# A decoder layer on one core: merge and output projection with tokens as rows and 512 weight columns as the moving side, attention values by tokens, and a ring of expert weights in three parts

## The chip, the core and the metric

The kernel runs on one core of a Trainium2 chip. The metric is the device time of one execution in microseconds. The engines are PE (TensorE, matrix products, with its weight loads shown apart as PEld), DVE (VectorE), ACT (ScalarE), POOL (GpSimd) and SP (SyncE, which here issues the DMA transfers). PSUM is the memory that products accumulate in.

## What is computed

One layer of a decoder with batch 1, 256 tokens and 1024 channels, in float32. Three token mixers run side by side, are merged by gates and projected; a mixture of 32 experts follows. Cut to what matters here:

```
cols = h @ w_in            # columns for the three mixers and three gates
y_a = rglru_branch(...)    # gated linear recurrence ("LRU")
y_b = stick_breaking_attention(q, k, v)      # 8 heads of 128
y_c = rwkv7_branch(...)    # delta-rule recurrence, 16 heads of 64
g_a, g_b, g_c = split(sigmoid(gate_logits))
merged = g_a * (y_a @ p_lru) + g_b * (y_b @ p_sb) + g_c * (y_c @ p_rwkv)
x = x + g_mix * (merged @ w_out)
h = modulate(rmsnorm(x), ...)
x = x + g_ffn * sum over the top 4 of 32 experts of
        weight * (clamped_swiglu(h @ w_gu[e]) @ w_down[e])
return rmsnorm(x)
```

The weights of the 32 experts are 384 MB (256 pieces of 1 MB for gate and up, 128 for down), those of everything ahead of them about 100 MB.

## The kernel before

All weights lie in DRAM in pieces that one DMA transfer brings in. `load` (L137) fetches one projection's weights of 1024 x 256 as two `raw` pieces of 512 KB each, into a pool of seven buffers (NRAW). A product with float32 accuracy is made of three: `split_w` (L146) splits a `raw` piece into a high part `whi` (a rounding copy on ACT, L149) and a low part `wlo` (a subtraction on DVE, L150), three buffers each (NSP); the activations come split as well (`hhi`/`hlo` for the normed input, `ybhi`/`yblo`, `yah`/`yal`, `ychi`/`yclo` for the three branches, `mh`/`ml` for the merged tile). high x high, high x low and low x high are then accumulated.

`proj` (L160) makes 256 output channels from 1024 input channels: the weights are the stationary operand (128 x 128), the 256 tokens move, 48 products (L168). The result has channels as partitions. Its accumulator is `mm`, one of three PSUM buffers of 512 columns (`pmm`, L157). `pch` (L175) gives one of three other buffers, `ch`; the rwkv recurrence and its output use these, and `tp` has two.

The program is written stage by stage: norm and adaLN, rwkv projections and the rwkv recurrence in two halves of 128 tokens, attention in four pairs of heads (`attention_pair`, L650), the LRU branch, the merge, output projection, router, experts. The written order is not the order in which an engine runs: a scheduler places each instruction ahead of time on its engine by data readiness, priorities and buffers that come free, with costs of its own; the engine then runs its list in that order and waits where an operand or a buffer isn't there. So the second half of the rwkv recurrence can stand, piece by piece, among the projections of other stages.

The second half's recurrence runs as follows, with the lines of its steps:
- 64-column triangular steps on DVE (L464, L465), a copy on ACT (L466), transposes on DVE (L469, L472);
- four groups of 32 x 32 products for the inverse blocks (L477, L483), copied by ACT and DVE (L479, L485);
- four steps over blocks of 32 tokens, each: `z` from the state and the block (L501, L504), its copy `rhs` on ACT (L507), `sps` on PE (L511), its copy `sav` on ACT (L512), `z` again and the state's update `nps` on PE (L515, L520), the copy `yt` on ACT (L529) and the new state `st` on DVE (L525 to L528);
- a group norm on DVE and ACT (L541 to L552), then for each of four column tiles two transposes (L557) and a product (L563) into `ch`, and three DVE operations that give `yc` (L559 to L564).

Attention (L611) turns the value tile of one head to tokens with two transposes and a DVE copy `vt`, as its values come out of `proj` with channels as partitions.

The merge (L860 to L891) runs over three branches (attention, LRU, rwkv) and four groups of 256 channels: gate projection from `hhi`/`hlo`, sigmoid on ACT into `gsig` (L878), projection of the branch, and a DVE product into `acc` (L881, or L883 and L884 for the later branches). In the third branch the sum is split into `mh`/`ml`. The output projection (L894 to L924) has four groups of 256 channels; there the merged tile is the stationary operand and the weights move, so that tokens are partitions; behind each group stand the gating and the residual add on DVE, the squares for the norm on ACT, and transposes and products for the router.

The experts' weights go through a ring of 19 buffers of 1 MB, opened in four parts of 7, 6, 3 and 3 (NR, L819; `ring_open`, L827) as the memory of earlier stages comes free. `ew_ahead` (L847) puts a few loads among those of the merge, in SP's queue. An expert makes `pg` and `pu` (L1043) on PE from gathered tokens `xe`, then the activation, then `pd` (L1070). At the end a count is read back (`values_load`, L1253), which decides whether a spare path must run.

Of the kernel before, what the change touches and what calls it, by code (L numbers as in the profile page):

```python
# [19 lines left out]
S = 256  # L20
# [60 lines left out]
def trace(tc, pools, I, out, dbg, stop):  # L81
# [63 lines left out]

    def split_w(src):  # L146

        hi, lo = (wsp.tile([128, 4, 256], F32R, name=n, tag=n, bufs=NSP) for n in ("whi", "wlo"))
# [501 lines left out]
    def attention_pair(pr):  # L650
        qkv = []
        for i, o in enumerate((OFF_Q, OFF_K, OFF_V)):
# [4 lines left out]
            ps = proj(raw, h2)  # L657
            A.activation(t, ps, AF.Copy, scale=128.0 ** -0.5 if i == 0 else 1.0)
            qkv.append(t)
        for cc in range(2):  # L660
            with sooner(HP_ATT):
                attention(pr * 2 + cc, *[t[:, cc] for t in qkv])
# [156 lines left out]
    NR = (7, 6, 3, 3)  # L819
    nload = [0]  # L820
# [18 lines left out]
    def ew(src):  # L839
        t = ew_tile()  # L840
        SY.dma_start(t.rearrange("p (k n) -> p k n", k=src.shape[1]), src)
# [15 lines left out]
    mhl, KS = None, 1  # L857
    EW = (0, 0, 1, 1, 1, 1, 1, 2)
    acc = [l4("acc") for _ in range(4)]
    for br, (yhl, pw) in enumerate(((ybhl, "p_sb"), (yahl, "p_lru"), (None, "p_rwkv"))):  # L860
        gcol = OFF_GATE + (1024, 0, 2048)[br]
# [5 lines left out]
        for pr in range(4):  # L867
            raw_g, raw_p = load(w_in, gcol + pr * 256), load(I[pw], pr * 256)
            if br:
                ew_ahead(EW[br * 4 + pr - 4])  # L870
            if br == 2 and pr == KS:
# [4 lines left out]
            c2 = slice(pr * 2, pr * 2 + 2)  # L876
# [3 lines left out]
            if br == 0:  # L880
                V.tensor_tensor(acc[pr], ps, sg, ALU.mult)  # L881
            else:
                V.tensor_tensor(sg, ps, sg, ALU.mult)  # L883
                V.tensor_tensor(acc[pr], acc[pr], sg, ALU.add)  # L884
            if br == 2:
                split_x(acc[pr], mhl[0][:, c2], mhl[1][:, c2])
                if pr == 3:
                    sqrt_ahead(sg)
# [4 lines left out]
    sqp = keep.tile([128, 2, 4], F32, name="sqp")  # L893
    lps = pch([128, 2, NE], "lps")  # L894
    for pr in range(4):
        raw = load(I["w_out"], pr * 256)
        ew_ahead(2 if pr < NR[1] - 4 else 1)
        ps = pmm().rearrange("p (t c) -> p t c", t=2)
        for q in range(2):
            hi, lo = split_w(raw[q])  # L900
            for t in range(2):
                for k in range(4):
                    for i, (w, x) in enumerate(((hi, 0), (hi, 1), (lo, 0))):
                        T.matmul(ps[:, t], mhl[x][:, q * 4 + k, t * 128:t * 128 + 128], w[:, k],
                                 start=(q + t + k + i == 0), stop=(q * 4 + k == 7 and i == 2), skip_group_check=True)
        if pr == 3:
# [3 lines left out]
        csl = slice(pr * 256, pr * 256 + 256)  # L910
        if pr == 2:
            gmix = mt("gmix", [128, 512])
            row_bcast(adag[:, 4:8], gmix)
        for t in range(2):
            V.tensor_tensor(ps[:, t], ps[:, t], gmix[:, pr % 2 * 256:pr % 2 * 256 + 256], ALU.mult)
# [412 lines left out]
```

## Time and profile before

| | us |
|---|---|
| Median of 3 runs | 1560.66 |
| Fastest and slowest run | 1560.38, 1562.57 |
| The profiled execution's own time | 1559.59 |
| Its span in the trace | 1557.8 |
| PE busy | 1455.1 (93%) |
| DVE busy | 643.3 (41%) |
| ACT busy | 413.3 (27%) |
| DMA moved | 498.87 MB, mean 320 GB/s |

The span is the time from the first to the last instruction of the profiled execution; some 2 us lie around it. The busy time of PE is a share of the whole; in the first 600 us and in the experts' part different things limit the kernel, so stretches are to be read one by one. A row of the timeline gives the start in us, the time it took, the engine, the line, the operation, output and inputs, and, in square brackets, for how long the engine had been idle and what released it.

### The profile page before, as it was taken

Reading aid. Unit: us, or ns where it says so; the run is one execution under the profiler, and the core shown is the slowest. Engines: PE = TensorE matmul, PEld = TensorE weight load, DVE = VectorE, ACT = ScalarE, POOL = GpSimd, SP = SyncE. Lnnn points to the kernel's source line nnn. Section 1 sums busy time; section 2 is a strip of 40 time slices with the busy share of each in tenths; the row PEclk is TensorE's granted clock in tenths of the full one; section 3 lists DMA queues with packets and bytes.
Section 4 is the critical chain, followed back from the end, with each engine's and each line's share of the span. In section 5 each row is a group of like instructions: output and inputs, shape, how many; then the busy total and the mean of one; then the engine's idle time right before and its main releaser. Section 6 shows DMA issues by size and latency. Waiting matters only on the chain. (4 is left out here: it accounts for less than half of the span.)

```text
span 1557.8 us, 21164 instructions
## 1 busy us (share of the span) xinstructions
PE 1455.1 (93%) x8608; PEld 830.7 (53%) x8608; DVE 643.3 (41%) x1330; ACT 413.3 (27%) x728; POOL 11.0 (1%) x59
## 2 busy tenths in 40 slices
PE   6998999899899998999999989999999989989896
PEld 4887989688899996334333324333323323323232
DVE  5678536589745764213232114213113113212313
ACT  4743335678534443001001001001001001001101
POOL 0000000000000000000000000000000000000000
PEclk8999799899899998999999999999999999999999
DMA  9554335246233777899999999999999999999994
GB/s 380 177 190 133 131 129 197 94 145 222 96 109 119 298 273 310 368 421 421 421 421 422 420 422 422 421 421 421 422 421 420 422 421 421 422 421 421 421 422 171
DMA packets 85558, 498.87 MB, mean 320 GB/s; under 512 B 12496, under 2 KB 12752, under 8 KB 36304
## 3 DMA queue, kind: packets, MB, share of 16 engines
q1 hardware_dynamic: 85456, 497.46, 80.0%
q8 instruction: 70, 1.15, 0.3%
q14 instruction: 32, 0.26, 0.0%
HBM read 496.37 MB, written 1.05 MB: 319 GB/s over the span
## 5 line engine op out<-in xcount | busy, mean ns | idle before, releaser
L1043 PE MATMUL pg<-ew,xe 128*64 128x512 f32 x1024 | 269.4, 603 | 25.2 <-DMA ew<-in_w_gu_dram 25.2
L1043 PE MATMUL pu<-ew,xe 128*64 128x512 f32 x1024 | 263.2, 595 | 0.0
L1070 PE MATMUL pd<-ew,act 128*64 128x512 f32 x992 | 231.6, 604 | 23.8 <-ACT act L1062 23.8
L168 PE MATMUL mm<-hhi,whi 128*128 128x256 f32 x720 | 212.6, 295 | 5.7 <-ACT gq L714 3.0
L168 PE MATMUL mm<-hhi,wlo 128*128 128x256 f32 x720 | 211.2, 293 | 1.1 <-DVE wlo L150 1.1
L168 PE MATMUL mm<-hlo,whi 128*128 128x256 f32 x720 | 211.7, 294 | 0.0
L150 DVE TENSOR_TENSOR wlo<-raw,whi 128x1024 fp32r<-128x1024 f32 x122 | 148.9, 1223 | 96.4 <-ACT whi L149 95.3
L149 ACT ACTIVATE whi<-raw 128x1024 fp32r<-128x1024 f32 x122 | 129.1, 1059 | 126.5 <-PE mm L168 94.4
L1043 PEld LDWEIGHTS pg<-ew,xe 128*64 128x64 f32 x1024 | 68.4, 137 | 174.1 <-issue 108.7
L1070 PEld LDWEIGHTS pd<-ew,act 128*64 128x64 f32 x992 | 69.7, 138 | 152.9 <-issue 116.0
L1043 PEld LDWEIGHTS pu<-ew,xe 128*64 128x64 f32 x1024 | 74.0, 137 | 143.3 <-issue 143.2
L168 PEld LDWEIGHTS mm<-hhi,whi 128*128 128x128 f32 x720 | 142.5, 198 | 12.8 <-issue 3.8
L168 PEld LDWEIGHTS mm<-hhi,wlo 128*128 128x128 f32 x720 | 142.2, 197 | 7.8 <-issue 5.2
L168 PEld LDWEIGHTS mm<-hlo,whi 128*128 128x128 f32 x720 | 142.3, 198 | 5.6 <-issue 4.8
L1076 DVE TENSOR_TENSOR yd<-pd,gff 128x512 f32<-128x512 f32 x31 | 21.5, 692 | 270.8 <-PE pd L1070 246.2
L1085 PE MATMUL pc<-yd,swt 64*128 64x512 f32 x248 | 96.0, 628 | 0.0
L1087 DVE TENSOR_TENSOR x<-x,pc 128x512 f32<-128x512 f32 x124 | 84.4, 683 | 11.7 <-PE pc L1085 10.7
L1085 PEld LDWEIGHTS pc<-yd,swt 64*128 64x128 f32 x248 | 30.1, 185 | 49.6 <-issue 28.8
L1015 ACT ACTIVATE xe<-xps,adaf,A 128x256 f32<-128x256 f32 x32 | 18.1, 565 | 101.3 <-DVE xe L1014 101.0
L1062 ACT ACTIVATE act<-act_ps 128x256 f32<-128x256 f32 x64 | 24.5, 383 | 72.2 <-PE act_ps L1060 71.0
L194 PE MATMUL adaps<-raw,crep 128*32 128x256 f32 x384 | 30.3, 433 | 9.9 <-DVE spt L579 9.1
L1014 DVE TENSOR_SCALAR xe<-xps,A,adaf 128x256 f32<-128x256 f32 x32 | 17.4, 544 | 44.4 <-PE xps L1011 44.4
(811 smaller groups left out, 1680.6 us busy)
## 6 DMA issues: line engine op xcount, KB each, us to landing
ew<-in_w_gu_dram SPq DMA_DIRECT2D x256, 1024.0 KB, 19.8
ew<-in_w_down_dram SPq DMA_DIRECT2D x128, 1024.0 KB, 19.8
raw<-in_w_in_dram SPq DMA_DIRECT2D x90, 512.0 KB, 4.2
raw<-in_w_ada_dram SPq DMA_DIRECT2D x32, 512.0 KB, 3.6
raw<-in_w_ada_dram SPq DMA_DIRECT2D x8, 1024.0 KB, 14.2
raw<-in_p_sb_dram SPq DMA_DIRECT2D x8, 512.0 KB, 4.1
raw<-in_p_lru_dram SPq DMA_DIRECT2D x8, 512.0 KB, 3.5
raw<-in_p_rwkv_dram SPq DMA_DIRECT2D x8, 512.0 KB, 5.4
```

Source lines behind the costliest of these rows:

```text
L149: A.activation(hi, src, AF.Copy)
L150: V.tensor_tensor(lo, src, r32(hi), ALU.subtract)
L168: T.matmul(ps[:, c], w[i][:, k, c * 128:c * 128 + 128], x[j][:, q * 4 + k], start=(q + c + k + n == 0), stop=(q == 1 and k == 3 and n == 2 ...
L194: T.matmul(ps[32 * j:32 * j + 32], crep[:, q * 4 + j, :], raw[q][:, j], start=(q == 0), stop=(q == 1))
L1014: V.tensor_scalar(xe[:, k, 0:n], xps[:, 0, 0:n], A2[:, k:k + 1], sh2[:, k:k + 1], ALU.mult, ALU.add)
L1015: A.activation(xe[:, k + 1, 0:n], xps[:, 1, 0:n], AF.Identity, scale=A2[:, k + 1:k + 2], bias=sh2[:, k + 1:k + 2])
L1043: i = T.matmul(p[hf * 64:hf * 64 + 64], xe[:, k], gu[k][:, c0:c0 + 512], start=False, stop=(k == KT - 1), skip_group_check=True)
L1062: A.activation(at, tp, AF.Copy)
L1070: i = T.matmul(pd[hf * 64:hf * 64 + 64], at[:, k % 2, (k // 4) * 64:(k // 4) * 64 + 64], w[:, hf * 512:hf * 512 + 512], start=(n == 0), st ...
L1076: V.tensor_tensor(yd, pd, gff2, ALU.mult)
L1085: T.matmul(ps, swt[sl, t], yd[sl], start=True, stop=True)
L1087: V.tensor_tensor(y[:, t, csl], y[:, t, csl], ps, ALU.add)
```

## The change

The diff does four things.

1. Merge and output projection are made by `proj_wide`: 512 output channels at a time, with the activations as the stationary operand (128 x 128) and 512 weight columns moving, for two token tiles of 128. `load_wide` brings the weights in four pieces of 512 KB. The gate's two accumulators are `gate` in the `mm` buffers, the branch projection's two are `pp` in the `ch` buffers. The merged tile now has tokens as partitions; it is turned with four transposes for each 512 channels and 128 tokens (`mt`) before its split.
2. Attention's values come from `proj_tok`, tokens as partitions, so that the two transposes and the copy for each head go.
3. The ring of expert weights is opened in parts of 8, 7 and 4 instead of 7, 6, 3 and 3; the loads that `ew_ahead` puts among those of the merge are distributed anew.
4. `values_load` is tied behind the last load of expert weights.

On the host, the weights are laid out in pieces for it.

```diff
+    def load_wide(src, i):
+        res = []
+        for q in range(4):
+            t = wraw.tile([128, 2, 512], F32, name="raw", tag="raw", bufs=NRAW)
+            last[0] = SY.dma_start(t.rearrange("p k n -> p (k n)"), src[i, q])
+            res.append(t)
+        return res
+    def proj_wide(raw, x, tiles):
+        for q in range(4):
+            w = split_w(raw[q])
+            for t in range(2):
+                for k in range(2):
+                    for n, (i, j) in enumerate(((0, 0), (1, 0), (0, 1))):
+                        T.matmul(tiles[t], x[i][:, q * 2 + k, t * 128:t * 128 + 128], w[j][:, k],
+                                 start=(q + k + n == 0), stop=(q == 3 and k == 1 and n == 2), skip_group_check=True)
+    def proj_tok(raw, x):
+        ps = pmm().rearrange("p (t c) -> p t c", t=2)
+        for q in range(2):
+            w = split_w(raw[q])
+            for t in range(2):
+                for k in range(4):
+                    for n, (i, j) in enumerate(((0, 0), (1, 0), (0, 1))):
+                        T.matmul(ps[:, t], x[i][:, q * 4 + k, t * 128:t * 128 + 128], w[j][:, k],
+                                 start=(q + t + k + n == 0), stop=(q == 1 and k == 3 and n == 2), skip_group_check=True)
+        return ps
...
-    def attention(hd, qs, ks, vc):
-        vt = a1("vt").rearrange("p (a t) -> p a t", a=2)
-        tp = ptp([128, 2, 128])
-        for t in range(2):
-            T.transpose(tp[:, t], vc[:, t * 128:t * 128 + 128], ident)
-        V.tensor_copy(vt, tp)
+    def attention(hd, qs, ks, vt):
...
-    NR = (7, 6, 3, 3)
-    nload = [0]
+    NR = (8, 7, 4)
+    nload, lastew = [0], [None]
...
-    EW = (0, 0, 1, 1, 1, 1, 1, 2)
-    acc = [l4("acc") for _ in range(4)]
+    EW = ((0, 0), (0, 1), (1, 1), (1, 1), (1, 1), (1, 0))
+    wide = lambda t: t.rearrange("p c t -> p (c t)")
+    acc = [wide(l4("acc")) for _ in range(4)]
...
-        for pr in range(4):
-            raw_g, raw_p = load(w_in, gcol + pr * 256), load(I[pw], pr * 256)
-            sg = g2("gsig")
-            A.activation(sg, proj(raw_g, h2), AF.Sigmoid)
-            ps = proj(raw_p, yhl)
+        for c in range(2):
+            raw_g = load_wide(I["w_gate"], (1, 0, 2)[br] * 2 + c)
+            ew_ahead(EW[br * 2 + c][0])
+            raw_p = load_wide(I[pw], c)
+            ew_ahead(EW[br * 2 + c][1])
+            pg = [pmm("gate") for _ in range(2)]
+            proj_wide(raw_g, h2, pg)
+            sg = [wide(g2("gsig")) for _ in range(2)]
+            for t in range(2):
+                A.activation(sg[t], pg[t], AF.Sigmoid)
+            pp = [pch([128, 512], "pp") for _ in range(2)]
+            proj_wide(raw_p, yhl, pp)
+            for t in range(2):
+                m = acc[c * 2 + t]
+                if br == 0:
+                    V.tensor_tensor(m, pp[t], sg[t], ALU.mult)
+                else:
+                    V.tensor_tensor(sg[t], pp[t], sg[t], ALU.mult)
+                    V.tensor_tensor(m, m, sg[t], ALU.add)
+                if br == 2:
+                    tp = pmm("mt").rearrange("p (j s) -> p j s", j=4)
+                    for j in range(4):
+                        T.transpose(tp[:, j], m[:, j * 128:j * 128 + 128], ident)
+                    split_x(tp, *[x[:, c * 4:c * 4 + 4, t * 128:t * 128 + 128] for x in mhl])
...
-    for pr in range(4):
-        raw = load(I["w_out"], pr * 256)
-        ew_ahead(2 if pr < NR[1] - 4 else 1)
-        ps = pmm().rearrange("p (t c) -> p t c", t=2)
+    for c in range(2):
+        raw = load_wide(I["w_out"], c)
+        ew_ahead(4 if c == 0 else NR[1] - 4)
+        ps = [pmm("xo") for _ in range(2)]
+        proj_wide(raw, mhl, ps)
...
-    most = nc.values_load(cnt_i, min_val=0, max_val=S)
+    with tc.issue_after(lastew[0].ins):
+        most = nc.values_load(cnt_i, min_val=0, max_val=S)
```

What the scheduler makes of it on the engines is seen at two places. The first is PE around the second half's recurrence. Before, at one of its steps (`z`, L515, and the state update `nps`, L520), products of a merge projection (`mm`, L168, from `ybhi`/`yblo`) stand on both sides:

```order
L168 MATMUL mm_4998<-ybhi_1465,whi_4999 128x256
L168 MATMUL mm_4998<-yblo_1466,whi_4999 128x256
L515 MATMUL z_3523<-sav_2725,gm_3269 64x64 x8
L520 MATMUL nps_3552<-sav_2725,bk_2724 128x128 x4
L168 MATMUL mm_4998<-ybhi_1465,wlo_5000 128x256
L168 MATMUL mm_4998<-ybhi_1465,whi_4999 128x256
L168 MATMUL mm_4998<-yblo_1466,whi_4999 128x256
```

Now on PE, from the last gate products (L188 is the product of `proj_wide`) into the recurrence; L508, L514, L535, L542, L546 and L551 are the lines that were L477, L483, L504, L511, L515 and L520, L734 belongs to the LRU branch:

```order
L188 MATMUL gate_4533<-wlo_4583,hhi_134 128x512
L734 MATMUL tp_4377<-xc_4372,lruw_2677 128x256 x2
L734 MATMUL tp_4390<-xc_4385,lruw_2677 128x256 x2
L508 MATMUL ch_3408<-au_3404,gm_3229 32x32 x16
L508 MATMUL ch_3426<-au_3404,gm_3229 32x32 x16
L514 MATMUL ch_3444<-gm_3229,au_3404 32x32 x16
L514 MATMUL ch_3462<-gm_3229,au_3404 32x32
L535 MATMUL z_3483<-sav_2685,gm_3229 128x64 x8
L514 MATMUL ch_3462<-gm_3229,au_3404 32x32 x15
L542 MATMUL sps_3494<-rhs_3492,gm_3229 64x64 x8
L546 MATMUL z_3483<-sav_2685,gm_3229 64x64 x8
L551 MATMUL nps_3512<-sav_2685,bk_2684 128x128 x4
```

And its end on PE, with the last output tiles of the recurrence (L588 the transposes, L594 the product) and the first products of a branch projection into `pp`:

```order
L594 MATMUL ch_3669<-sgx_352,gup_2681 128x256
L588 MATMUL ch_3672<-ident_82,yt_3480 128x128 x2
L594 MATMUL ch_3678<-sgx_352,gup_2681 128x256
L588 MATMUL ch_3681<-ident_82,yt_3480 128x128 x2
L594 MATMUL ch_3687<-sgx_352,gup_2681 128x256
L188 MATMUL pp_4602<-whi_4604,ybhi_1465 128x512
L188 MATMUL pp_4602<-whi_4604,yblo_1466 128x512
```

Between the first of these two pieces and the second PE's list holds the remaining three steps of the recurrence and its output, and no product of `proj_wide`.

The second place is DVE at the same steps. Before, the splits of merge weights (`wlo`, L150) and a product into `acc` (L881) stand among the recurrence's operations:

```order
L485 TENSOR_SCALAR gm_3269<-ch_3484 32x16x32
L485 TENSOR_SCALAR gm_3269<-ch_3502 32x16x32
L150 TENSOR_TENSOR wlo_5067<-raw_5056,whi_5066 128x1024
L528 TENSOR_TENSOR st_3521<-nps_3552,pend_2765 64x4x64 x2
L150 TENSOR_TENSOR wlo_5095<-raw_5058,whi_5094 128x1024
L881 TENSOR_TENSOR acc_4555<-mm_4998,gsig_4939 128x512
L150 TENSOR_TENSOR wlo_5125<-raw_5060,whi_5124 128x1024
```

Now DVE has these rows at that place (L516, L559, L556, L557 and L572 were L485, L528, L525, L526 and L541):

```order
L516 TENSOR_SCALAR gm_3229<-ch_3444 32x16x32
L516 TENSOR_SCALAR gm_3229<-ch_3462 32x16x32
L559 TENSOR_TENSOR st_3481<-nps_3512,pend_2725 64x4x64 x2
L556 TENSOR_TENSOR st_3481<-nps_3553,st_3481 64x4x64 x2
L557 TENSOR_TENSOR st_3481<-st_3481,pend_2725 64x4x64 x2
L556 TENSOR_TENSOR st_3481<-nps_3596,st_3481 64x4x64 x2
L557 TENSOR_TENSOR st_3481<-st_3481,pend_2725 64x4x64 x2
L572 TENSOR_REDUCE mean_3640<-yt_3480 128x16
```

The splits moved out of the recurrence, to places ahead of it and behind it.

## Rows read from the trace of the kernel before

**Rows 1.** Stretches: us; busy us of each engine (instructions); PE clock, DMA share, GB/s.

```profile
610.00:615.00 5.00, 5.00 (x27) 3.48 (x26) 1.09 (x2) 1.13 (x2) 0.00 (x0) 0.80 0.00 0
700.00:1500.00 800.00, 748.41 (x3291) 264.23 (x3289) 204.30 (x460) 77.66 (x193) 0.00 (x0) 0.99 1.01 421
```

**Rows 2.** Timeline of SP's queue, two issues of expert weights (start, us).

```profile
614.30 0.33 SPq L841 DMA_DIRECT2D ew<-in_w_gu_dram  x1
...
640.13 3.67 SPq L841 DMA_DIRECT2D ew<-in_w_gu_dram  x3
```

**Rows 3.** Timeline of PE: last output projection product, first and last expert gate products.

```profile
597.66 0.28 PE L904 MATMUL mm<-wlo,mh 128*128 128x256 f32 x1
...
612.32 1.08 PE L1043 MATMUL pg<-ew,xe 128*64 128x512 f32 x4
...
1528.50 1.08 PE L1043 MATMUL pg<-ew,xe 128*64 128x512 f32 x4 [0.55 <-DMA ew<-in_w_gu_dram]
```

**Rows 4.** Timeline of PE: products of 256 columns, and of 512 columns.

```profile
535.07 0.28 PE L168 MATMUL mm<-hhi,wlo 128*128 128x256 f32 x1
...
537.87 0.28 PE L168 MATMUL mm<-hhi,wlo 128*128 128x256 f32 x1
...
622.36 1.03 PE L1043 MATMUL pg<-ew,xe 128*64 128x512 f32 x4
623.22 1.03 PE L1043 MATMUL pu<-ew,xe 128*64 128x512 f32 x4
```

**Rows 5.** Timeline of all engines from 416 to 434.5 us, the recurrence's beginning.

```profile
416.97 1.23 DVE L150 TENSOR_TENSOR wlo<-raw,whi 128x1024 fp32r<-128x1024 f32 x1 [0.48 <-ACT whi L149]
...
418.55 0.17 DVE L465 TENSOR_TENSOR xb<-xb,subt 128x16 f32<-128x16 f32 x1
...
420.25 0.68 ACT L466 ACTIVATE xb<-xb 64x512 f32<-64x512 f32 x1
...
420.96 2.27 DVE L469 STREAM_TRANSPOSE au<-xb 32x1024 f32<-32x1024 f32 x1
...
424.64 2.21 PE L477 MATMUL ch<-au,gm 32*32 32x32 f32 x64
...
430.73 2.00 PE L504 MATMUL z<-sav,gm 64*128 64x64 f32 x16
...
433.82 0.68 DVE L485 TENSOR_SCALAR gm<-ch 32x512 f32<-32x512 f32 x1 [1.50 <-PE ch L483]
```

**Rows 6.** Timeline of all engines from 447 to 463 us, one step.

```profile
447.40 0.38 PE L501 MATMUL z<-st,qr 128*128 128x128 f32 x2
...
451.47 0.59 ACT L507 ACTIVATE rhs<-z 64x512 f32<-64x512 f32 x1 [1.71 <-PE z L504]
...
455.97 1.14 PE L511 MATMUL sps<-rhs,gm 64*64 64x64 f32 x16
...
461.26 1.16 PE L520 MATMUL nps<-sav,bk 128*128 128x128 f32 x8
...
462.45 0.88 DVE L525 TENSOR_TENSOR st<-nps,st 64x256 f32<-64x256 f32 x2 [0.20 <-PE nps L520]
```

**Rows 7.** Timeline of all engines from 497 to 519 us, group norm and output.

```profile
497.36 1.22 DVE L541 TENSOR_REDUCE mean<-yt 128x16 f32<-128x1024 f32 x1 [0.31 <-ACT yt L529]
...
505.28 1.28 DVE L552 TENSOR_TENSOR yt<-yt,var 128x512 f32<-128x512 f32 x2
...
509.67 0.54 DVE L559 TENSOR_SCALAR yc<-ch,pc 128x256 f32<-128x256 f32 x1
510.25 0.42 DVE L561 TENSOR_TENSOR yc<-yc,bv 128x256 f32<-128x256 f32 x1
...
517.43 0.59 PE L563 MATMUL ch<-sgx,gup 128*128 128x256 f32 x2
```

**Rows 8.** Stretch in the first half's recurrence, columns as in rows 1.

```profile
168.00:182.00 14.00, 14.00 (x119) 13.09 (x116) 7.71 (x9) 3.98 (x8) 0.00 (x0) 0.51 0.28 85
```

**Rows 9.** Timeline of PE from 168 to 182 us.

```profile
173.90 3.67 PE L504 MATMUL z<-sav,gm 64*128 64x64 f32 x16
```

More of the change, by code (lines that the diff above doesn't have):

```diff
@@ L144, in load @@
         return res
+    def load_wide(src, i):
[5 more added lines that the diff above has]
+        return res
     def split_w(src):
-        hi, lo = (wsp.tile([128, 4, 256], F32R, name=n, tag=n, bufs=NSP) for n in ("whi", "wlo"))
+        hi, lo = (wsp.tile(list(src.shape), F32R, name=n, tag=n, bufs=NSP) for n in ("whi", "wlo"))
         A.activation(hi, src, AF.Copy)
@@ L661, in attention_pair @@
             with sooner(HP_ATT):
-                attention(pr * 2 + cc, *[t[:, cc] for t in qkv])
+                attention(pr * 2 + cc, qkv[0][:, cc], qkv[1][:, cc], qkv[2][:, :, cc * 128:cc * 128 + 128])
     R1 = 4
@@ L840, in ew @@
         t = ew_tile()
[L841 removed]
+        lastew[0] = SY.dma_start(t.rearrange("p (k n) -> p k n", k=src.shape[1]), src)
         return t
@@ L889, in trace @@
+            if br == 2 and c == 1:
+                sqrt_ahead(sg[1])
     pools.close(mg, mixer)
     ring_open()
-    sqp = keep.tile([128, 2, 4], F32, name="sqp")
+    sqp = keep.tile([128, 2, 2], F32, name="sqp")
     lps = pch([128, 2, NE], "lps")
-    for pr in range(4):
-        raw = load(I["w_out"], pr * 256)
-        ew_ahead(2 if pr < NR[1] - 4 else 1)
-        ps = pmm().rearrange("p (t c) -> p t c", t=2)
[L899 to L906, printed above, removed]
+    for c in range(2):
[3 more added lines that the diff above has]
+        proj_wide(raw, mhl, ps)
+        if c == 1:
@@ L909, in trace @@
             ew_ahead(NR[2])
-        csl = slice(pr * 256, pr * 256 + 256)
-        if pr == 2:
             gmix = mt("gmix", [128, 512])
             row_bcast(adag[:, 4:8], gmix)
+        csl = slice(c * 512, c * 512 + 512)
         for t in range(2):
-            V.tensor_tensor(ps[:, t], ps[:, t], gmix[:, pr % 2 * 256:pr % 2 * 256 + 256], ALU.mult)
-            V.tensor_tensor(x1[:, t, csl], x1[:, t, csl], ps[:, t], ALU.add)
-            A.activation(ps[:, t], x1[:, t, csl], AF.Square, accum_out=sqp[:, t, pr:pr + 1])
-            tp = ptp([128, 2, 128])
-            for kk in range(2):
-                T.transpose(tp[:, kk], x1[:, t, (pr * 2 + kk) * 128:(pr * 2 + kk + 1) * 128], ident)
-            xt = mt("x1t", [128, 2, 128], 2, "swt")
-            V.tensor_copy(xt, tp)
-            for kk in range(2):
-                T.matmul(lps[:, t], xt[:, kk], wr[:, pr * 2 + kk], start=(pr + t + kk == 0), stop=(pr * 2 + kk == 7),
-                         skip_group_check=True)
+            V.tensor_tensor(ps[t], ps[t], gmix, ALU.mult)
+            V.tensor_tensor(x1[:, t, csl], x1[:, t, csl], ps[t], ALU.add)
+            A.activation(ps[t], x1[:, t, csl], AF.Square, accum_out=sqp[:, t, c:c + 1])
+            for h in range(2):
+                tp = ptp([128, 2, 128])
+                for kk in range(2):
+                    k = c * 4 + h * 2 + kk
+                    T.transpose(tp[:, kk], x1[:, t, k * 128:k * 128 + 128], ident)
+                xt = mt("x1t", [128, 2, 128], 2, "swt")
+                V.tensor_copy(xt, tp)
+                for kk in range(2):
+                    k = c * 4 + h * 2 + kk
+                    T.matmul(lps[:, t], xt[:, kk], wr[:, k], start=(t + k == 0), stop=(k == 7), skip_group_check=True)
     dump("x1", x1)
@@ L1302, in layout @@
     res = {"x": a["x"][0], "pc": np.ascontiguousarray(pc), "b_router": a["b_router"]}
-    for n in ("p_lru", "p_sb", "p_rwkv", "w_out", "w_in", "w_ada"):
-        res[n] = pieces(a[n][0], 256, 2)
+    res["w_in"], res["w_ada"] = pieces(a["w_in"][0][:, :OFF_GATE], 256, 2), pieces(a["w_ada"][0], 256, 2)
+    res["w_gate"] = pieces(a["w_in"][0][:, OFF_GATE:], 512, 4)
+    for n in ("p_lru", "p_sb", "p_rwkv", "w_out"):
+        res[n] = pieces(a[n][0], 512, 4)
     res["w_down"] = np.ascontiguousarray(a["w_down"][0].reshape(NE, 4, 2, 128, D).transpose(0, 1, 3, 2, 4)).reshape(NE, 4, 128, 2 * D)
```

20 lines of the change are left out of this document (3 added, 17 removed).

## Prediction, made before the changed kernel ran

> **What bounds the kernel now.** I read the stretches of the program first, then the issues of the expert weights, then the first and last expert products. In [rows 1] the stretch from 700 to 1500 us runs with the DMA engines full (share 1.01, 421 GB/s) while TensorE is only about as busy as the data lets it be; the last gate product still waits for its weights at 1528.50 [rows 3]. So the expert stage is a stream of 384 pieces of 1 MB, and its end is set by when the stream runs freely. Before that the ring of 19 pieces is full: DMA moves nothing from 610 to 615 us [rows 1], and piece 19 (counting from 0) goes out at 614.30 [rows 2], 2.0 us after the first expert product at 612.32 [rows 3] has begun to empty a buffer. The next gap in the stream, before the issue at 640.13 [rows 2], is again a wait for the first expert's work. Hence the rule of my sum: with all 19 pieces loaded in time, every microsecond by which the first expert product moves moves the end by a microsecond. That product lies at the end of a chain on TensorE: attention, the LRU branch, merge, output projection (last product at 597.66, [rows 3]), then 14.4 us of norm, routing and gather.
>
> **Products of 512 columns.** Merge and output projection are 24 + 4 projections of 48 products of 256 columns (1344); they become 12 + 2 of 48 products of 512 (672). From 535.07 to 537.87 lie 24 starts of 256-column products [rows 4], 0.117 us each, 157 us for 1344. No 512-column product with 128 stationary columns runs in a row in this trace; the nearest are the experts' (64 columns): from 622.36 to 623.22, 0.86 us, four start [rows 4], 0.2145 each. By that row 672 cost 144.1 us, a gain of 13 us. The other bound is twice the 256-column interval, 0.234, and no gain. I take 0.2145, the same moving width.
>
> **Attention by tokens.** It removes 16 transposes on PE and 8 copies on DVE and leaves the products at the same count and width. Transposes at the pace of products [rows 4] give 16 x 0.117 = 1.9 us; I take 2.
>
> **What moves: the recurrence loses its cover.** This is the large term. The rwkv recurrence is a chain PE, ACT, PE, ACT, PE, DVE. Before, its pieces lie between merge projections, so that PE never waits for it: the step of [rows 6] can take its time under them (the next product of the chain starts at 455.97, 3.9 us after its operand was ready, 451.47 + 0.59). In the new order, shown with the change, PE has one gate projection, then the whole second half's recurrence and its output, and only then the first product into a "pp" tile; DVE and ACT hold no merge split in between either. The reason is the accumulator: "pp" comes from the three "ch" buffers, which the recurrence and its output hold until their last tiles are read, while before merge used "mm" alone. PE works in program order, so it must idle through this chain.
>
> When it begins: the last triangular step on DVE ends at 418.72 [rows 5]. In the new order DVE has 7 merge splits ahead of it, not 13, and neither of the two products into acc (512 columns, 0.68 by the L485 row [rows 5], 1.4 together); a split is 1.23 us (416.97, [rows 5]). 418.7 - 6 x 1.23 - 1.4 - 2 (attention) = 408. Then ACT 0.68 and the transpose 2.27 [rows 5]: PE starts at 411.1 (with hops of 0.15). The single gate projection ahead of it (48 x 0.2145 = 10.3 us) ends long before: its four splits stand ahead of the LRU branch and of the last triangular steps in DVE's order.
>
> How long it takes, bare, at full clock, from rows:
> Inverse blocks: products of L477 and L483, the latter taken as long as the former, the first z of L504, a DVE copy and hops: 2.21 + 2.21 + 2.00 + 0.68 + 0.2 = 7.3 [rows 5].
> One middle step [rows 6]: z from 447.40 to the start of rhs at 451.47, 4.07 with its hop; rhs 0.59; sps 1.14; the same ACT copy 0.59; L515 (as long as sps) and L520 together 2.2; two pairs on DVE 0.88 and 0.88; the other hops, some 0.5: 10.8. Two of them 21.7. The first step has no z: 5.4. The last has no state update: 8.5.
> Group norm: 9.2 us from 497.36 to 505.28 + 1.28 [rows 7], with two merge splits of 1.23 among it on DVE, which partly hide ACT's square root; about 7 without.
> Output: one column tile is 0.54 + 2 x 0.42 on DVE, with hops 1.5 [rows 7]; pp's first buffer is free after the third: two transposes and the first product, 0.9, and 3 x 1.5, together 5.4.
> Sum 55.3 us at 2.4 GHz.
>
> The clock. In the first half's own recurrence, where tiny products (32 and 64 columns) stand alone, the granted clock was 0.51 from 168 to 182 us [rows 8]; that is the 1.2 GHz level. The 16 products of L504 took 3.67 us there [rows 9] and 2.00 at full clock [rows 5], a factor 1.83. In the new order nothing but such products and waits stands on PE for the whole chain. With all its PE parts (about 32 us of the 55.3) at that factor it is 82 us. I take 73, two thirds of the way: the low level is the likelier one by the first half, but no row of before shows the second half's chain bare. So pp begins at 411.1 + 73 = 484.1.
>
> **After it.** 13 projections (one pp, five pairs, two of the output) x 48 x 0.2145 = 133.9. Other work on PE in this stretch (gff, row broadcasts, router transposes): in the order of before, 576 products of 0.117 (67.4 us) follow the recurrence's last column tile, which ends about 518.6 (517.43 for the third [rows 7], half a us for the fourth); to 597.66 + 0.28 [rows 3] are 79.3 us, so 11.9 of other work, which stays. The merged tile must now be turned: 16 transposes (2 us) and, for each half, a wait of 1.5 us for the DVE add ahead of them (3 us); that is 5. The clock may stay low for a while after the chain: between nothing and 7 us (half of a stretch as long as that of [rows 8]); I take 3. Together 153.8, and the last projection ends at 637.9. The tail then: DVE has twice the columns behind the last product, and ACT half the squares; I take 15 instead of 14.4. First expert product 652.9 instead of 612.3: +40.6 us.
>
> **What costs nothing.** The ring's parts (8, 7, 4 for 7, 6, 3, 3) are 19 either way, and both have landed before the first expert product. The x1, router and bias loads stand in SP's queue ahead of the last two p_sb pieces and wait for yc; PE needs those pieces 10 us later. The load of the count is taken out of SP's queue ahead of piece 19; SP would have waited for the buffer until 614.3 anyway; if that cover went, at most some 3 us return. DMA needs 41 MB after yc, about 100 us at 421 GB/s, in 150 us.
>
> **The sum.** Profiled execution 1559.59 + 40.6 = 1600.2; the median of before is 1.07 above its profiled execution, so 1601.
>
> **Rivals.**
> Full clock in the chain: 55.3 instead of 73 and no recovery gives 1601 - 20.7 = 1580. Against it: the first half's own recurrence [rows 8]. Chance 0.16.
> Products at twice the 256-column interval: 13 x 48 x 0.0195 = 12 us, 1613. It would need a cost that doubles with the width; the experts' rows speak against it. 0.05.
> The chain stays covered (faster): if the order did not bind PE, or the chain were ready before PE comes to it, what remains is 13 + 2 - 5 = 10 us of gain, 1551. The DVE row that ends at 418.72 would have to be 55 us earlier. 0.04.
> 512-column products that cost no more than the interval of the weight loads, 0.117 (faster): 624 x 0.0975 = 61 us less, 1540. The experts' rows are at 0.2145 with the same width, so 0.02. The Trainium skill, "TensorE: Matmul & The Clock Gate", section "Back-to-back issue gap", gives about 131 ns for a product of 512 columns in a sustained stream of pairs with weight loads, and calls 216 ns too high. By 131 the 624 products would be 52 us shorter and the time about 1549, faster than before; this trace does not agree, its experts' products start 0.86 / 4 us apart, 215 ns [rows 4].
> The delay is absorbed (no change): if the stream of weights were ahead by more than the ring holds, 1561. Against it the 5 us without any DMA at 610 [rows 1]. 0.03.
>
> **How the numbers follow.** Forecast 1601, 0.70. A measurement of this kernel can tell about 0.2%, 3 us. Slower 0.70 + 0.16 + 0.05 = 0.91, faster 0.06, same 0.03. The range takes in the full clock at the bottom, with 5 us for the start of the chain (1575), and at the top a chain wholly at the low clock (+8.9, 1610) with half of the wide products' bound (+6): 1616.
>
> **What would show it.** In the changed profile: a stretch of some 70 us near 411 to 484 with PE half idle, clock near 0.5, and waits of PE for ACT and DVE at the recurrence's lines; then products of 512 columns 0.215 us apart with PE full; first expert product near 653; after it the same stream at 421 GB/s. I am wrong if PE shows merge products inside the recurrence, if the first expert product comes before 615, or if the expert stage is shorter than 916 us from first to last gate product.

## The result, and the profile of the changed kernel

The changed kernel takes 1598.53 us (median of 4 runs, 1597.32 to 1602.01). Its ratio to the kernel before is 1.0265, with a 95% interval of 1.0232 to 1.0298: slower by some 40 us (41 by the ratio; the medians, 1561.62 of 4 runs before, lie 36.9 apart). 1601 us had been forecast, within 1575 to 1616.

The profiled execution has a span of 1596.7 us, 38.9 more than before. The page's second part cuts it into 40 slices of 39.9 us; here are PE's busy share, its granted clock (both in tenths) and the DMA share:

```profile
PE   7999999994879998999999999999989999989896
PEclk8999999996559999899999999999999999999999
DMA  9455443442007758599999999999999999999994
```

Slices 10 to 12 (359 to 479 us) are the change: PE is busy for 4, 8 and 7 tenths, its clock falls to 0.6 and 0.5, and DMA stands at nothing in two of them. Before, PE was busy for 9, 8 and 9 tenths there. The same as a row of stretches (us; busy us of PE, PEld, DVE, ACT, POOL with instruction counts; clock, DMA share, GB/s), over the second half's rwkv recurrence:

```profile
395.00:472.00 77.00, 59.59 (x384) 50.39 (x382) 18.38 (x31) 11.12 (x18) 0.00 (x0) 0.50 0.00 1
```

For 77 us PE works at 1.2 GHz on small products only, DVE is busy for 18 us and ACT for 11: each of the three waits for the others in turn. The timeline of PE shows where that begins and ends, and what follows (start, us, then the instruction, in brackets the idle time before it and its releaser):

```profile
361.37 0.40 PE L188 MATMUL gate<-whi,hhi 128*128 128x512 f32 x1
...
366.04 0.40 PE L188 MATMUL gate<-wlo,hhi 128*128 128x512 f32 x1
...
394.79 3.62 PE L508 MATMUL ch<-au,gm 32*32 32x32 f32 x64 [16.62 <-DVE au L500]
...
400.47 3.67 PE L535 MATMUL z<-sav,gm 64*128 64x64 f32 x16
...
472.27 0.79 PE L188 MATMUL pp<-whi,ybhi 128*128 128x512 f32 x1
...
629.67 0.39 PE L188 MATMUL xo<-wlo,mh 128*128 128x512 f32 x1
...
632.39 0.39 PE L188 MATMUL xo<-wlo,mh 128*128 128x512 f32 x1
...
650.90 1.08 PE L1074 MATMUL pg<-ew,xe 128*64 128x512 f32 x4
```

After the gate products PE has an LRU step (L734) and then waits 16.6 us for the recurrence's first operand. The recurrence and its output take from 394.79 to 472.27, 77.5 us, and only then comes the first product into `pp`. The 16 products at L535 (L504 before) take 3.67 us, as in the first half [rows 9], not 2.00 [rows 5]. The last output product starts at 632.39, the first expert product at 650.90, where before it was 612.32 [rows 3]: 38.6 later, and the span is longer by 38.9.

DVE's timeline shows how bare the chain is:

```profile
391.77 0.17 DVE L496 TENSOR_TENSOR xb<-xb,subt 128x16 f32<-128x16 f32 x1
...
412.46 0.88 DVE L559 TENSOR_TENSOR st<-nps,pend 64x256 f32<-64x256 f32 x2 [5.87 <-PE nps L551]
427.98 0.87 DVE L556 TENSOR_TENSOR st<-nps,st 64x256 f32<-64x256 f32 x2 [14.65 <-PE nps L551]
428.89 0.87 DVE L557 TENSOR_TENSOR st<-st,pend 64x256 f32<-64x256 f32 x2
444.41 0.88 DVE L556 TENSOR_TENSOR st<-nps,st 64x256 f32<-64x256 f32 x2 [14.65 <-PE nps L551]
```

From the second state update to the third are 16.4 us (427.98 to 444.41), of which DVE waits 14.65 for PE. The row at 391.77, the last triangular step, answers to the one at 418.55 [rows 5]: it comes 26.8 us earlier, which the forecast had put at 10.7 (418.7 to 408).

### The profile page after: what moved, and what is told of

It is laid out like the page before. It is cut to its first block, busy times and chain, and to the rows that moved or that the text cites. A ratio compares the mean times of both kernels' runs of the same rounds, so it can differ in the third digit from the quotient of the medians.

```text
span 1596.7 us, 19792 instructions
## 1 busy us (share of the span) xinstructions
PE 1466.2 (92%) x7936; PEld 810.3 (51%) x7936; DVE 639.5 (40%) x1314; ACT 411.1 (26%) x720; POOL 9.6 (1%) x59
## 5 line engine op out<-in xcount | busy, mean ns | idle before, releaser
L1074 PE MATMUL pu<-ew,xe 128*64 128x512 f32 x1024 | 267.1, 593 | 0.0
L177 PE MATMUL mm<-hhi,whi 128*128 128x256 f32 x464 | 135.2, 292 | 0.7 <-DVE kx L358 0.7
L177 PE MATMUL mm<-hhi,wlo 128*128 128x256 f32 x464 | 134.8, 291 | 0.5 <-DVE wlo L159 0.4
L177 PE MATMUL mm<-hlo,whi 128*128 128x256 f32 x464 | 134.2, 289 | 0.0
L1107 DVE TENSOR_TENSOR yd<-pd,gff 128x512 f32<-128x512 f32 x31 | 21.4, 692 | 246.1 <-PE pd L1101 227.2
L177 PEld LDWEIGHTS mm<-hhi,wlo 128*128 128x128 f32 x464 | 89.6, 193 | 6.1 <-issue 4.3
L177 PEld LDWEIGHTS mm<-hlo,whi 128*128 128x128 f32 x464 | 89.7, 193 | 5.1 <-issue 4.7
L177 PEld LDWEIGHTS mm<-hhi,whi 128*128 128x128 f32 x464 | 89.6, 193 | 5.3 <-issue 3.1
L188 PE MATMUL gate<-whi,hhi 128*128 128x512 f32 x96 | 38.4, 401 | 0.0
```

Of the source, the lines that this page charges most:

```text
L188: T.matmul(tiles[t], x[i][:, q * 2 + k, t * 128:t * 128 + 128], w[j][:, k], start=(q + k + n == 0), stop=(q == 3 and k == 1 and n == 2), s ...
L1074: i = T.matmul(p[hf * 64:hf * 64 + 64], xe[:, k], gu[k][:, c0:c0 + 512], start=False, stop=(k == KT - 1), skip_group_check=True)
L1107: V.tensor_tensor(yd, pd, gff2, ALU.mult)
```

## Experiments

Each ratio is to the kernel before, run on the same chip at the same time. The kernel before itself went from 1550 to 1567 us in these runs, so ratios with their intervals count, and times of the profiled executions only show where things lie.

### pp_mm: the accumulator named back

```diff
-            pp = [pch([128, 512], "pp") for _ in range(2)]
+            pp = [pmm("pp") for _ in range(2)]
```

> The changed kernel with one word changed: the branch projection's two accumulators pp come from the three mm buffers instead of the three ch buffers. In its order on PE the second half's recurrence again stands piece by piece among the products of gate and pp. Theory 1 (the recurrence lost its cover because pp shares ch with it): the stretch of 77 us at clock 0.50 is gone, first expert product between 612 and 630 us instead of 650.90, time 1560 to 1578; what keeps it above the kernel before is the turn of the merged tile, the longer tail and the wait for a third mm buffer. Rival (the cover went because pieces of 512 columns are too coarse, whatever the buffer): time stays near 1598.

Measured: 1554.06 us, ratio 0.9976 (0.9948 to 1.0003). The rival falls. PE's timeline at one step of the recurrence:

```profile
448.70 0.66 PE L535 MATMUL z<-sav,gm 64*128 64x64 f32 x4
449.29 0.50 PE L188 MATMUL gate<-wlo,hhi 128*128 128x512 f32 x1
...
454.02 0.39 PE L188 MATMUL pp<-whi,yal 128*128 128x512 f32 x1
454.33 1.14 PE L542 MATMUL sps<-rhs,gm 64*64 64x64 f32 x16
```

Between the `z` products and `sps` stand 21 products of 512 columns again, and the chain's products are at full clock: `sps` takes 1.14 us as in [rows 6]. Over the stretch in which the recurrence runs, the row is

```profile
400.00:530.00 130.00, 128.14 (x773) 102.91 (x771) 74.52 (x100) 54.10 (x72) 1.13 (x1) 0.97 0.42 138
```

with PE busy for 128 of 130 us at 0.97. The first expert product comes at 608.48, 42 us earlier than in the changed kernel. One accumulator's name is the cause of the loss; pieces of 512 columns hide the recurrence as those of 256 did. I had put what remains of the change's own cost above the kernel before; it came out at or below it, since attention gives more than I thought (below). The wide merge and output projection, as a whole, gain nothing even so: `narrow` (below), run beside `pp_mm` and without them, is faster, with a mean of 1548.7 us against 1554.4, a difference of 5.6 with an interval of some 4 us to either side. PE's two longest waits from 360 to 610 us are:

```profile
PE pp L188 <- ACT gsig L909: 6.0, 1, 6.0
PE tp L986 <- DVE sel L982: 4.5, 1, 4.5
```

(in all us, times, longest). The first is a wait for the sigmoid that empties a gate buffer, as expected of three buffers for gate and `pp`; the second is for the router's selection in the tail, and no matter of these buffers.

### ch_narrow: the reverse, in the kernel before

```diff
-    def proj(raw, x):
+    def proj(raw, x, acc=None):
...
+        ps = (acc or pmm)().rearrange("p (c t) -> p c t", c=2)
...
-            ps = proj(raw_p, yhl)
+            ps = proj(raw_p, yhl, lambda: pch([128, 512], "pp"))
```

> The kernel before with one change: the branch projections of the merge (256 columns, as before) accumulate in the three ch buffers instead of the mm buffers. In its order on PE the second half's recurrence then stands alone, ahead of the first product into pp, as in the changed kernel. Theory 1 (the shared ch buffers alone uncover the chain): a stretch of 70 to 80 us at clock 0.50 without projections, ratio to the kernel before 1.025 to 1.04 (1600 to 1622). Rival (the uncovering needs the 512-column pieces too): ratio below 1.01.

Measured: 1612.58 us, ratio 1.0355 (1.0315 to 1.0394), as the theory said. With 256-column products, the old attention and the old ring, the name alone costs 3.5%. The stretch and the rows of PE at its ends and at the first expert product:

```profile
395.00:490.00 95.00, 60.76 (x388) 50.89 (x386) 31.96 (x68) 22.66 (x35) 0.00 (x0) 0.52 0.02 6
```

```profile
412.39 3.62 PE L477 MATMUL ch<-au,gm 32*32 32x32 f32 x64 [16.80 <-DVE au L469]
...
489.89 0.58 PE L168 MATMUL pp<-ybhi,whi 128*128 128x256 f32 x1
...
664.32 1.88 PE L1043 MATMUL pg<-ew,xe 128*64 128x512 f32 x4
```

From 412.39 to 489.89 are 77.5 us, the same as in the changed kernel.

### dummy and dummy2: what the clock costs in the chain

Both add products that nothing uses to the changed kernel, in the recurrence's second half, where PE waits: `dummy` 2, 2 and 5 in a step, `dummy2` 1, 1 and 2 (the edit shown is that of `dummy2`).

```diff
+        def idle(n, after, dst):
+            if b == 0:
+                return
+            with tc.issue_after(after.ins):
+                for _ in range(n):
+                    T.matmul(dst[64:128].rearrange("p a h i -> p (a h i)"), bv[:, 0, 0:64],
+                             bv[:, 0:2].rearrange("p k t -> p (k t)"), start=True, stop=True, skip_group_check=True)
...
+            idle(1, m, spw)
             A.activation(sav[0:64, :, c], sps.rearrange("p a h i -> p a (h i)"), AF.Copy)
...
+                idle(2, m, spw)
```

> The changed kernel with 9 needless products (64 stationary, 512 moving columns, plain float32, into an unused half of sps) in each of the four steps of the second half's recurrence, placed on PE where it waits for ACT or DVE; outputs don't use them. Between 395 and 470 us the changed kernel's granted clock is 0.50 and a middle step takes 16.4 us. Theory (the low clock costs some 20 us of the bare chain, and comes of PE's little work there): the clock rises in the steps, a step takes 11 to 14 us, first expert product 8 to 20 us earlier than 650.9, time 1579 to 1591. Rival (the clock doesn't follow, or the chain's time is its hops): the added products only delay, 1600 to 1620.

Measured: 1613.12 us, ratio 1.034 (1.0298 to 1.0382): slower than the changed kernel. The clock did follow, as the stretch from 430 to 450 us shows, but a step isn't shorter:

```profile
430.00:450.00 20.00, 19.32 (x97) 10.15 (x95) 1.69 (x4) 1.77 (x3) 0.00 (x0) 1.00 0.00 1
```

```profile
432.39 0.49 PE L541 MATMUL z<-st,qr 128*128 128x128 f32 x2
...
436.40 1.93 PE L534 MATMUL sps<-bv 128*64 128x512 f32 x4
...
444.10 4.51 PE L534 MATMUL sps<-bv 128*64 128x512 f32 x10
448.54 0.49 PE L541 MATMUL z<-st,qr 128*128 128x128 f32 x2
```

16.15 us a step against 16.4 without them. An added product has two records (4 for two products, 10 for five), and nine products fill 1.93 + 1.93 + 4.51 = 8.4 us, more than the waits that they were put into; what the clock gave, the added work took. The chain also began 13 us later in this profile (407.88), before any of the added products; the order of PE is the same up to there, so that isn't the edit's doing. From its first product to the first into `pp` (490.44) the chain takes 82.6 us, 5 more than without them; the rest of the difference lies ahead of it.

> As dummy, with 4 needless products in a step instead of 9 (1 while rhs and 1 while sav is copied, 2 while the state is updated), so that they fit under the waits. In dummy the clock rose to 1.00 and a step's own parts took what I had priced at full clock (z loop 4.07, L553 1.14), but the added products took 8.4 us of the step's 16.2. If the clock holds: a step of 11 to 12.5 us, from the recurrence's first product to the first into pp 60 to 66 us instead of 77.5, and the time some 10 us under the changed kernel's, ratio 1.015 to 1.022. If the clock falls back to 0.50 with so little added: step 16 to 18 us, ratio 1.025 or more.

Measured: 1596.82 us, ratio 1.0264 (1.0209 to 1.0319). The stretch of the two middle steps, and the first products of each and of the last:

```profile
422.00:456.00 34.00, 31.66 (x206) 19.81 (x204) 3.37 (x8) 4.79 (x9) 0.00 (x0) 0.99 0.00 1
```

```profile
422.92 0.49 PE L541 MATMUL z<-st,qr 128*128 128x128 f32 x2
...
434.95 0.46 PE L541 MATMUL z<-st,qr 128*128 128x128 f32 x2
...
446.95 0.46 PE L541 MATMUL z<-st,qr 128*128 128x128 f32 x2
```

The clock holds at 0.99 and a step takes 12.0 us instead of 16.4, in the bounds given. The whole chain takes 71.0 us (398.35 to 469.31) instead of 77.5, not the 60 to 66 expected: its first 22 us, up to the first state update at 419.92, had a clock of 0.50, and the norm and the output behind the steps (456 to 469 us) one of 0.65. And the time isn't resolved from that of the changed kernel, where a ratio of 1.015 to 1.022 had been expected: the 6.5 us won in the chain lie within the intervals, and in the profile the chain began 3.6 us later. So the low clock does cost 4 us a step, and goes when PE has four products more in each; as a remedy that is worth little beside covering the chain.

### probe: the pace of 512-column products

Six runs of 48 products are put between merge and output projection of the changed kernel (60 us more work).

```diff
+    for f, name in enumerate(("prall", "prone", "prhalf", "przero", "prnar", "prlow")):
...
+        for n in range(48):
...
+            T.matmul(ps[0:m, 0:w], st, mv, start=(n == 0), stop=(n == 47), skip_group_check=True)
```

> The changed kernel with six runs of 48 products put between merge and output projection (some 60 us more time): fp32r, 128 stationary columns and 512 moving (prall), the same with one stationary tile for all (prone), with 64 stationary columns (prhalf), with moving zeros (przero), with 256 moving columns (prnar), with the low part stationary (prlow). In the changed kernel the 512-column products start every 0.233 us (gate, pp) and 0.227 (xo), where I had taken 0.2145. If it is the number of stationary columns, prhalf comes near 0.2145 and the others stay; if the change of the stationary tile, prone does; if the data, przero does and prlow differs from prall; if it is a cost of each product, twice prnar is more than prall.

One run: 1660.27 us. PE's timeline:

```profile
608.62 11.44 PE L940 MATMUL prall<-hhi,mh 128*128 128x512 f32 x48
619.90 11.36 PE L940 MATMUL prone<-hhi,mh 128*128 128x512 f32 x48
631.10 11.25 PE L940 MATMUL prhalf<-hhi,mh 128*64 128x512 f32 x48
642.18 11.09 PE L940 MATMUL przero<-zero,mh 128*128 128x512 f32 x48
653.11 5.76 PE L940 MATMUL prnar<-hhi,mh 128*128 128x256 f32 x48
658.71 11.36 PE L940 MATMUL prlow<-hhi,ml 128*128 128x512 f32 x48
```

From start to start, divided by 48: 0.235 us, 0.233 with one stationary tile, 0.231 with 64 stationary columns, 0.228 with zeros, and 0.1167 with 256 columns. None of the suspects brings 0.2145; twice the narrow product is the wide one. The 2 to 3% by zeros is the only difference of note, but `xo` runs at 0.227 without zeros. Why the pace is 0.233 and not 0.2145 is so answered the other way round: 0.2145 was no pace of a product. The page's group of the experts' gate products shows it:

```profile
L1074 PE MATMUL pg<-ew,xe 128*64 128x512 f32 x1024 | 272.2, 599 | 22.7 <-DMA ew<-in_w_gu_dram 22.5
```

32 experts times 8 pieces times 2 halves are 512 products into `pg`, but 1024 records. These operands are declared plain float32 (those of the merge F32R; both read f32 in the rows), each product has two records, and two products with 64 stationary columns each stand side by side. "Four in 0.86 us" [rows 4] are two products that run together: in the trace they start at 622.357 and 622.364 us, then at 622.786 and 622.793, one record of each product at a time.

### narrow: the change without its wide products

Merge and output projection as before; attention by tokens, the ring of 8, 7 and 4 and the late load of the count kept.

```diff
+    NR = (8, 7, 4)
...
+    EW = (0, 0, 1, 1, 1, 1, 2, 2)
```

> The changed kernel without its first part: merge and output projection as before (256 columns), but attention values by tokens, ring in parts of 8, 7, 4 and the late load of the count. My theory: these parts together give 2 us by 16 transposes less, 1558 to 1560 against 1560.7. Rival (one of them costs, by the ring's parts or by SP's queue): 1563 or more.

Measured: 1549.59 us, ratio 0.9939 (0.9914 to 0.9965): faster, by 9.5 us instead of 2. The first expert product comes at 597.35, 15.0 us before that of [rows 3].

### att_only and no_tok: attention by tokens alone, and its removal

`att_only` is the kernel before with `proj_tok` and without the transposes and the copy of each head; `no_tok` is the changed kernel with them put back.

```diff
-            ps = proj(raw, h2)
+            ps = proj_tok(raw, h2) if i == 2 else proj(raw, h2)
```

> The kernel before with attention values by tokens alone. In the narrow kernel attention ended at 262.3 us instead of 275.9 and the first expert product came 15.0 us earlier, where I had priced 2 us for 16 transposes. Theory (the whole of that gain comes from attention: transpose and copy stood in each head's chain, and with them PE waits and loses clock between 140 and 210 us): like narrow, a ratio of 0.992 to 0.996 to the kernel before. Rival (the ring's parts or the late load of the count gave it): ratio 0.998 to 1.000, attention's end near 274.

> The changed kernel with attention's values as before (two transposes and a copy for each head); all else as changed. If attention by tokens is worth 13 to 18 us in this kernel, as the end of attention suggests (257.4 against 275.9), the time is 1608 to 1616. If it is worth the 2 us of its transposes, 1600.

Measured: `att_only` 1546.32 us, ratio 0.9922 (0.9894 to 0.9949), the lowest ratio of this study. `no_tok` 1616.74 us, ratio 1.0349 (1.0300 to 1.0398), against 1.0265 for the changed kernel. So attention by tokens is worth 12 us (0.0078 x 1559, with an interval of 4 to either side) in the one and 13 us (0.0084 x 1559, with some 9 to either side) in the other, six times what I gave it. Ring and late load add nothing that shows: `narrow` and `att_only` have overlapping intervals.

The stretch from 130 to 210 us, where attention meets the first half's recurrence, in the kernel before, in `no_tok`, in `att_only` and in the changed kernel, in this order:

```profile
130.00:210.00 80.00, 75.30 (x645) 66.44 (x644) 43.47 (x101) 26.03 (x43) 0.40 (x6) 0.81 0.45 153
```

```profile
130.00:210.00 80.00, 74.75 (x638) 65.28 (x637) 42.86 (x99) 25.91 (x43) 0.40 (x6) 0.81 0.46 158
```

```profile
130.00:210.00 80.00, 78.83 (x765) 70.75 (x763) 49.75 (x112) 31.55 (x52) 0.52 (x8) 0.98 0.55 185
```

```profile
130.00:210.00 80.00, 78.83 (x764) 70.62 (x763) 49.52 (x111) 32.75 (x55) 0.52 (x8) 0.98 0.53 178
```

With the transposes, PE does some 640 instructions in 80 us at a clock of 0.81; without, 765 at 0.98. Other kernels don't divide so by the clock. Here are `narrow` and `pp_mm`, without the transposes, and `ch_narrow`, with them:

```profile
130.00:210.00 80.00, 78.78 (x733) 70.42 (x731) 47.92 (x107) 31.07 (x51) 0.52 (x8) 0.91 0.50 173
```

```profile
130.00:210.00 80.00, 79.43 (x715) 71.18 (x714) 47.16 (x108) 29.62 (x49) 0.52 (x8) 0.87 0.51 174
```

```profile
130.00:210.00 80.00, 74.66 (x691) 66.75 (x690) 48.71 (x115) 28.37 (x47) 0.54 (x8) 0.89 0.47 159
```

What divides all seven is PE's busy time in these 80 us: 74.7 to 75.3 with the transposes, 78.8 to 79.4 without. The clock differs between executions of one order as well (last section), so its part in the 12 us isn't shown.

### att_extra, att_tp and att_copy: what of the transposes costs

All three start from `att_only` and put unused work on the keys `ks` back into each head: two transposes and a copy, the transposes alone, or a copy alone.

```diff
+        ex = a1("ex").rearrange("p (a t) -> p a t", a=2)
+        tp = ptp([128, 2, 128])
+        for t in range(2):
+            T.transpose(tp[:, t], ks[:, t * 128:t * 128 + 128], ident)
+        V.tensor_copy(ex, tp)
```

> Attention values by tokens alone (as in att_only), but with two transposes and a DVE copy for each head put back, of the keys and unused, so that nothing waits for them. Theory (the gain of 12 us came from where the transposes stood: each head's chain waited for them and the first half's recurrence met an idle PE and a clock of 0.81 between 130 and 210 us): ratio 0.993 to 0.996, clock there 0.95 or more. Rival (the instructions themselves cost it): ratio 0.998 to 1.002, clock there 0.81 to 0.85.

Measured: 1560.68 us, ratio 1.0023 (1.0003 to 1.0043). My theory falls: nobody waits for these transposes, and the whole gain is gone. The clock from 130 to 210 us, 0.87, met neither of the two bounds named; PE was busy for 74.9 of the 80 us, as in the kernels that have the transposes.

> att_only with two unused transposes of the keys for each head into a tp buffer, without the DVE copy. att_extra (transposes and copy, nobody waiting) gave back all of the gain, so the instructions cost it. In att_extra's and this kernel's order heads 3 to 7 stand later against the first half's recurrence than in att_only's. Theory 2 (the two tp buffers, through which each head also passes its scores, are what an additional tile takes): ratio 0.998 to 1.004, like att_extra. Rival (DVE's 8 copies): ratio 0.990 to 0.996, like att_only.

> att_only with one unused DVE copy of the keys (128 x 256) for each head, without the transposes; its order on PE is att_only's. Theory 2 (tp buffers): ratio 0.990 to 0.996, like att_only. Rival (DVE's copies): 0.998 to 1.004.

Measured: `att_tp` 1.0006 (0.9984 to 1.0029), `att_copy` 0.9959 (0.9934 to 0.9984). The transposes carry most of the price, with or without a copy behind them. The copies cost little: `att_copy` lies at the upper end of what was said, and its interval overlaps that of `att_only` (its profiled execution was the slowest of its runs, 1561.8 against a median of 1551.35, so its trace isn't used). By [rows 4] the 16 transposes are 2 us of PE; the rest comes with the place in the `tp` buffers that they take, or with the order that the scheduler then makes: heads 3 to 7 stand later against the first half's recurrence. These two go together here.

### att_yp: one more tile out of the tp buffers

```diff
-        yp = ptp([128, S])
+        yp = pmm("yp")[:, 0:S]
```

> att_only with one more tile taken out of the two tp buffers: each head's output yp accumulates in an mm buffer. Theory 2 taken further (tp buffers are what attention waits for): attention ends before 260 us, ratio to the kernel before 0.980 to 0.991, below att_only's 0.992. Rival (with the values' transposes gone, tp is no longer short; mm, which the projections need, becomes so): 0.992 to 1.000.

Measured: 1567.47 us, ratio 1.0072 (1.0042 to 1.0102): a miss, slower than the kernel before and outside what theory and rival had said. PE's waits between 110 and 300 us:

```profile
PE tp L647 <- DVE beta L644: 10.6, 2, 6.7
PE ch L495 <- DVE gm L484: 1.6, 1, 1.6
```

The first line is two waits of PE for the scores of a head, 10.6 us together; the longest of `att_only` in this window is 2.2. So "fewer tiles in `tp`" is no rule by itself; whether the loss comes of the `mm` buffers that `yp` takes or of the order that was then made isn't shown. Whether buffers or order made the 12 us stays open.

## Why the forecast held, and which of its terms didn't

**The rule of the end held in each kernel.** From the first expert product to the end of the span are 945.5 us before (612.32, 1557.8), 945.8 in the changed kernel, 946.7 in `pp_mm` (608.48, 1555.2), 946.4 in `narrow` (597.35, 1543.7) and 947.5 in `ch_narrow` (664.32, 1611.8). What is late ahead of the experts is late at the end, and what is early is early.

**The mechanism held.** PE's idle chain, its reason (`pp` in the `ch` buffers) and its size were as forecast, and `pp_mm` and `ch_narrow` show the reason from both sides. The rival with full clock in the chain (1580) is out: the clock was 0.50 throughout, and `dummy2` shows what full clock would be, 12.0 us a step with some products added, where 10.8 had been worked out without them. The rival in which the chain stays covered needed one word (`pp_mm`).

**Two terms of the sum were mis-sized, in opposite directions.** The sum, term by term, in us:

| term | forecast | measured |
|---|---|---|
| PE begins the recurrence | 411.1 | 394.79 |
| chain to the first product into pp | 73 | 77.5 |
| from there to the end of the last output product | 153.8 | 160.5 (to 632.39 + 0.39) |
| of it 13 projections of 48 products | 133.9 | 145.1 (528 x 0.2335 + 96 x 0.2267) |
| of it other work, turn, recovery | 19.9 | 15.4 |
| tail to the first expert product | 15 | 18.1 |
| first expert product | 652.9 | 650.90 |

The first: *attention by tokens*, taken as 2 us, is worth 12 to 13. I counted the removed transposes at PE's pace and looked no further; they stand in a stretch where PE, with them, is busy for some 4 us less in 80, and cost six times their own time; by which way stays open. The recurrence began 16.3 us earlier than forecast, and it is attention that brings it forward: in the profile of `no_tok`, its slowest run, it begins at 416.22, 21.4 us later than in the changed kernel, and so the rest of the change, DVE's shorter list with it, gives 8.4 (424.64 to 416.22).

The second: *products of 512 columns*, taken as 13 us of gain, give next to none. 0.2335 us (20 intervals from 361.37 to 366.04) is twice the 0.117 of [rows 4], and `xo` with 0.2267 (12 intervals from 629.67 to 632.39) gains 3%. That is the rival "twice the 256-column interval", which I gave 0.05 because of the experts' rows; those rows were two products side by side. The Trainium skill's figure ("TensorE: Matmul & The Clock Gate", section "Back-to-back issue gap", 131 ns for 512 columns in a sustained stream) is not borne out either: no form of the probe is below 227 ns.

The chain ran wholly at the low clock: 77.5 against the 73 that I had taken between 55 and 82, so that the 82 worked out for just this case was 4.5 too long. The other work was 4.5 less, since the clock was back with the third product into `pp` and the turn's waits were short; the tail was 3.1 more. PE's waits there:

```profile
PE mt L922 <- DVE acc L918: 2.9, 2, 1.5
PE tp L952 <- DVE x L946: 2.7, 1, 2.7
```

The first is the turn of the merged tile (3 us had been put down for it), the second the wider residual add in the tail.

So the time was right to 2.5 us with errors of 16 and 11 us in it that nearly cancelled; that closeness is luck. Had the pace been right and attention as I took it, I would have said 1612 (1601 + 11); with attention right and the pace wrong, 1585 (1601 - 16). Both lie in the range.

**What was said to cost nothing** did: ring parts and the late load of the count don't show in `narrow` against `att_only`.

## What to carry to other kernels

Before an accumulator is moved into other buffers, ask who holds those buffers and for how long: a chain that was free because other products filled its waits becomes the longest thing in the kernel when those products need its buffers, and its own products then run at the low clock besides. A pace should be taken from a row of the same operand type and the same number of stationary columns, and the number of records checked against the number of products in the code. And a small step that is removed from a tight stretch is not priced by its own duration; measure it alone, as here, where it was the only part of the change that gained, and alone gives the lowest ratio (`att_only`, 0.9922).

## What the runs showed of the hardware that I had not expected

- The granted clock differs between executions of the same order. The changed kernel, `probe`, `dummy2` and `dummy` have the same list on PE up to the recurrence; from 130 to 210 us their profiles show 0.98, 0.98, 0.94 and 0.89, and the recurrence begins at 394.79, 394.29, 398.35 and 407.88 us.
- With a few added products between the small ones the granted clock stayed at full: with four in a step 0.99 (`dummy2`, 422 to 456 us), without them 0.50 (395 to 472).
- F32R products cost by their moving columns alone here: 0.117 us for 256, 0.233 for 512, with 128 or 64 stationary columns; zeros as moving data ran 2 to 3% faster. A plain float32 product of 512 columns has two records; two such products one behind the other take 1.9 us (`dummy`), two with 64 stationary columns each, side by side, 0.86 [rows 4].
